# A 64 KB store of zeros ahead of the loads, in place of an early 1 MB store

## The chip, the cores and the metric

The kernel runs on one core of a Trainium2 chip. Of the core's engines it uses VectorE (DVE) for all arithmetic on the large tensors, ScalarE (ACT) for two small activations, and the queues of SyncE (SP) and ScalarE to issue DMAs; sixteen DMA engines move the data between HBM and the on-chip memory. The metric is the device time of one execution in microseconds (us), as the median over several runs. A profiled execution has besides a span, from the first to the last thing that the profiler recorded.

## The reference

```python
batch, seq, hidden, n_experts, k = 16, 1024, 512, 8, 2
...
logits_max = np.max(router_logits, axis=-1, keepdims=True)
probs = np.exp(router_logits - logits_max)
probs = probs / np.sum(probs, axis=-1, keepdims=True)
topk_indices = np.argsort(probs, axis=-1)[..., -k:]
topk_probs = np.take_along_axis(probs, topk_indices, axis=-1)
topk_probs = topk_probs / np.sum(topk_probs, axis=-1, keepdims=True)
x_expanded = x[:, :, np.newaxis, :].repeat(k, axis=2)
return (x_expanded * topk_probs[..., np.newaxis]).astype(np.float32)
```

For each of 16,384 tokens the two largest of eight router logits are turned into two weights that sum to one, and the token's 512 float32 values are written out twice, once times each weight. So 33.55 MB of x and 0.52 MB of logits are read, and 67.11 MB are written.

## The kernel before

The tokens are laid out with 128 of them on each of 128 partitions (M = 128): partition p holds tokens 128p to 128p + 127. A "row" below is one token index m on all 128 partitions. One row of x is 2 KB on each partition, and one row of the output is 4 KB on each partition.

The logits come in with one DMA (L72). `top2_weights` finds the largest and the second largest of the eight logits with a tree of maxima and minima on DVE (L26 to L36), takes their difference (L39), and two sigmoids on ACT (L41, L42) give both weights for all rows, in the tile WA.

Then two groups of 64 rows are handled one after the other (L93). For each group the SP queue issues four loads of 16 rows, 4 MB each, into the tile xs (L96), and then a plan of seven entries is walked through (L83 to L91). Each entry is one multiplication on DVE (L99), which writes n rows times both weights, and one store of those rows (L107). Where the product goes differs: rows 0 to 15 go to a second tile, osp, in two parts of e = 2 and 14 rows; rows 16 to 31 overwrite the lower half of xs, whose rows are by then used up; rows 32 to 47 go to osp again in two halves, which must first have been stored; rows 48 to 63 overwrite the upper half of xs.

Nothing is double-buffered beyond this. The loads of the second group overwrite xs, so two of them wait for the store of its lower half, and the other two for the stores of its upper half. All DMAs are issued from the SP queue, in program order, with one exception: the very first store, of rows 0 and 1 of the first group (1 MB), goes out on the ACT queue (L106). In the second group the same two rows are stored from the SP queue. A DMA's arrival is signalled by a semaphore, and the framework adds the waits on it: before an instruction that reads or overwrites a tile, before a store to output bytes that an earlier store wrote, and, since there are eight such semaphores, before the ninth DMA reuses the first one's.

Of the kernel before, what the change touches and what calls it, by code (L numbers as in the profile page):

```python
# [1 line left out]

# [4 lines left out]

F32 = mybir.dt.float32
ALU = mybir.AluOpType
ACTF = mybir.ActivationFunctionType  # L10
P = 128


def top2_weights(nc, pool, logits, M, E):

    hi, lo, n = None, None, E
    while n > 1:  # L20
        n //= 2
        if hi is None:
            a, b = logits[:, :, 0:n], logits[:, :, n : 2 * n]
            nhi = pool.tile([P, M, n], F32, tag=f"hi{n}")
            nlo = pool.tile([P, M, n], F32, tag=f"lo{n}")
            nc.vector.tensor_tensor(nhi, a, b, op=ALU.max)  # L26
            nc.vector.tensor_tensor(nlo, a, b, op=ALU.min)  # L27
        else:
            a, b = hi[:, :, 0:n], hi[:, :, n : 2 * n]
            nhi = pool.tile([P, M, n], F32, tag=f"hi{n}")  # L30
            nlo = pool.tile([P, M, n], F32, tag=f"lo{n}")
            tmp = pool.tile([P, M, n], F32, tag=f"tmp{n}")
            nc.vector.tensor_tensor(tmp, lo[:, :, 0:n], lo[:, :, n : 2 * n], op=ALU.max)  # L33
            nc.vector.tensor_tensor(nlo, a, b, op=ALU.min)  # L34
            nc.vector.tensor_tensor(nlo, nlo, tmp, op=ALU.max)  # L35
            nc.vector.tensor_tensor(nhi, a, b, op=ALU.max)  # L36
        hi, lo = nhi, nlo
    dlt = pool.tile([P, M], F32, tag="dlt")
    nc.vector.tensor_tensor(dlt, hi[:, :, 0], lo[:, :, 0], op=ALU.subtract)  # L39
    WA = pool.tile([P, M, 2], F32, tag="WA")  # L40
    nc.scalar.activation(WA[:, :, 0], dlt, ACTF.Sigmoid, scale=-1.0)  # L41
    nc.scalar.activation(WA[:, :, 1], dlt, ACTF.Sigmoid, scale=1.0)  # L42
    return WA


@with_exitstack
def kernel(
    ctx: ExitStack,
    tc: tile.TileContext,
    x: bass.AP,  # L50
    router_logits: bass.AP,
    k: bass.AP,
    out: bass.AP,
):
    nc = tc.nc
    B, S, D = x.shape
    E = router_logits.shape[-1]
    N = B * S
    assert int(k) == 2 and E == 8 and N % P == 0
    M = N // P  # L60

    GROUP = 64
    L = 16
    x_v = x.rearrange("b s d -> (b s) d").rearrange("(p m) d -> p m d", p=P)
    o_v = out.rearrange("b s k d -> (b s) k d").rearrange("(p m) k d -> p m k d", p=P)
    rl_v = router_logits.rearrange("b s e -> (b s) e").rearrange(
        "(p m) e -> p m e", p=P
    )

    wpool = ctx.enter_context(tc.tile_pool(name="wpool", bufs=1))  # L70
    logits = wpool.tile([P, M, E], F32)
    nc.sync.dma_start(logits, rl_v)  # L72
    WA = top2_weights(nc, wpool, logits, M, E)

    xs = wpool.tile([P, GROUP, D], F32)
    osp = wpool.tile([P, L, 2, D], F32)


    low = xs[:, : 2 * L, :].rearrange("p (r k) d -> p r k d", k=2)
    high = xs[:, 2 * L :, :].rearrange("p (r k) d -> p r k d", k=2)  # L80
    h = L // 2
    e = 2
    plan = [  # L83
        (0, e, osp[:, :e]),
        (e, L - e, osp[:, e:]),
        (L, L, low),
        (2 * L, h, osp[:, :h]),
        (2 * L + h, h, osp[:, h:]),
        (3 * L, h, high[:, :h]),
        (3 * L + h, h, high[:, h:]),  # L90
    ]  # L91

    for g in range(M // GROUP):  # L93
        m0 = g * GROUP
        for r in range(0, GROUP, L):
            nc.sync.dma_start(xs[:, r : r + L, :], x_v[:, m0 + r : m0 + r + L, :])  # L96
        for r, n, og in plan:
            rows = slice(m0 + r, m0 + r + n)
            nc.vector.tensor_tensor(  # L99
                og,  # L100
                xs[:, r : r + n, :].unsqueeze(2).to_broadcast([P, n, 2, D]),
                WA[:, rows, :].unsqueeze(3).to_broadcast([P, n, 2, D]),
                op=ALU.mult,
            )

            queue = nc.scalar if rows.start == 0 else nc.sync  # L106
            queue.dma_start(o_v[:, rows], og)  # L107


# [1 line left out]
_INS = ['x', 'router_logits', 'k']  # L111
_OUTS = [((16, 1024, 2, 512), 'float32')]

_NUMBERS = {'k': 2}


# [26 lines left out]
```

## Time and profile before

| | |
|---|---|
| Time, median of 6 runs | 242.74 us |
| The six runs | 241.92, 242.01, 242.70, 242.78, 242.79, 242.91 us |
| The profiled execution, time | 241.89 us |
| The profiled execution, span | 240.1 us |
| DVE busy | 142.1 us (59% of the span), 25 instructions |
| ACT busy | 1.8 us, 3 instructions |
| DMA, mean rate over the span | 421 GB/s, 101.19 MB |
| HBM read, written | 34.08 MB, 67.11 MB |

The profile names a group of instructions by its line, its engine and the tiles it writes and reads, as in "L99 DVE osp<-xs,WA". q1 is the SP queue's ring of DMA work and q10 the ACT queue's; both feed the same sixteen DMA engines. "Issue to landing" is the time from the issuing instruction to the last semaphore event of a DMA, so it includes what stands ahead of the DMA in its ring. A DMA is cut into packets; in this kernel a packet is one contiguous piece on one partition, and each of the sixteen engines handles eight partitions, so every DMA of 128 partitions is eight packets on each engine and a semaphore packet of 4 bytes. The trace keeps every packet's start, length in bytes and duration.

### The profile page before, as it was taken

To read this page: it belongs to the slowest core of one execution; us is meant where nothing else is said; L and a number is where in the kernel's file an instruction comes from. 1 tells how busy PE (TensorE), PEld (TensorE's weight loads), DVE (VectorE), ACT (ScalarE), POOL (GpSimd) and SP (SyncE) were. 2 spreads that over 40 slices of the span, in tenths; PEclk is the share of its full clock that TensorE was granted. 3 is DMA by queue.
4 is the path that set the end of the run, shared out by engine and by line. 5 is a ranking of instruction groups with operands and counts; after the bars stand their busy time and mean duration, and the time that the engine had idled before them with its cause. 6 is when DMAs were issued, how large, how long until landed. Compare 5 with 4: busy or idle time off the path is not lost.

```text
span 240.1 us, 116 instructions
## 1 busy us (share of the span) xinstructions
DVE 142.1 (59%) x25; ACT 1.8 (1%) x3; POOL 0.2 (0%) x4
## 2 busy tenths in 40 slices
DVE  2369999910499999300000999997007999990000
ACT  2000000000000000000000000000000000000000
POOL 0000000000000000000000000000000000000000
DMA  6999999989989899999999999989989898999996
GB/s 262 437 437 393 459 426 437 513 353 411 502 371 502 349 437 437 437 437 437 437 349 437 437 437 437 437 343 524 420 383 513 349 524 349 437 437 437 437 437 262
DMA packets 3312, 101.19 MB, mean 421 GB/s; under 512 B 368, under 2 KB 368, under 8 KB 496
## 3 DMA queue, kind: packets, MB, share of 16 engines
q1 hardware_dynamic: 3168, 100.14, 97.6%
q10 hardware_dynamic: 144, 1.05, 1.0%
HBM read 34.08 MB, written 67.11 MB: 421 GB/s over the span
## 4 chain that ended last, share of the span: by engine, by line
DMA 49%; DVE 32%; issue 7%; SPq 1%; DVEq 0%
DMA out_dram<-osp 26%; DMA xs<-in_x_dram 23%; DVE osp L99 18%; DVE xs L99 14%; SPq L96 0%; SPq L72 0%; SPq L107 0%; DVEq L99 0%
## 5 line engine op out<-in xcount | busy, mean ns | idle before, releaser
L99 DVE TENSOR_TENSOR osp<-xs,WA 128x8192 f32<-128x8192 f32 (+2 forms) x8 | 69.2, 8687 | 69.2 <-DMA xs<-in_x_dram 40.4
L99 DVE TENSOR_TENSOR xs<-xs,WA 128x8192 f32<-128x8192 f32 (+1 forms) x6 | 69.2, 11536 | 0.2
L26 DVE TENSOR_TENSOR nhi<-logits 128x512 f32<-128x512 f32 x1 | 0.7, 691 | 4.5 <-DMA logits<-in_router_logits_dram 4.5
L41 ACT ACT_TABLE_LOAD x1 | 1.3, 1283 | 0.7 <-PEq L124 0.7
L33 DVE TENSOR_TENSOR tmp<-nlo 128x256 f32<-128x256 f32 (+1 forms) x2 | 0.7, 352 | 0.0
L34 DVE TENSOR_TENSOR nlo<-nhi 128x256 f32<-128x256 f32 (+1 forms) x2 | 0.7, 352 | 0.0
L36 DVE TENSOR_TENSOR nhi<-nhi 128x256 f32<-128x256 f32 (+1 forms) x2 | 0.7, 352 | 0.0
L35 DVE TENSOR_TENSOR nlo<-nlo,tmp 128x256 f32<-128x256 f32 (+1 forms) x2 | 0.7, 352 | 0.0
L27 DVE TENSOR_TENSOR nlo<-logits 128x512 f32<-128x512 f32 x1 | 0.7, 684 | 0.0
L41 ACT ACTIVATE WA<-dlt 128x128 f32<-128x128 f32 x1 | 0.3, 315 | 6.2 <-DVE dlt L39 6.2
L39 DVE TENSOR_TENSOR dlt<-nhi,nlo 128x128 f32<-128x128 f32 x1 | 0.3, 292 | 0.0
L42 ACT ACTIVATE WA<-dlt 128x128 f32<-128x128 f32 x1 | 0.3, 298 | 0.0
L124 POOL MEMSET const-bfloat16-1.0<- 128x1 bf16 x1 | 0.1, 102 | 0.0
L124 POOL MEMSET const-uint8-127<- 128x1 uint8 x1 | 0.1, 102 | 0.0
L124 POOL MEMSET const-float32-1.0<- 128x1 f32 x1 | 0.1, 99 | 0.0
L124 POOL MEMSET const-float32-0.0<- 128x1 f32 x1 | 0.1, 98 | 0.2 <-issue 0.2
## 6 DMA issues: line engine op xcount, KB each, us to landing
xs<-in_x_dram SPq DMA_DIRECT2D x8, 4096.0 KB, 36.7
out_dram<-osp SPq DMA_DIRECT2D x4, 4096.0 KB, 20.7
out_dram<-xs SPq DMA_DIRECT2D x4, 4096.0 KB, 22.7
out_dram<-osp SPq DMA_DIRECT2D x2, 7168.0 KB, 31.6
out_dram<-osp ACTq DMA_DIRECT2D x1, 1024.0 KB, 16.2
out_dram<-osp SPq DMA_DIRECT2D x1, 1024.0 KB, 29.7
logits<-in_router_logits_dram SPq DMA_DIRECT2D x1, 512.0 KB, 3.7
out_dram<-xs SPq DMA_DIRECT2D x2, 33.6
```

What stands on the lines that cost most here:

```text
L26: nc.vector.tensor_tensor(nhi, a, b, op=ALU.max)
L27: nc.vector.tensor_tensor(nlo, a, b, op=ALU.min)
L33: nc.vector.tensor_tensor(tmp, lo[:, :, 0:n], lo[:, :, n : 2 * n], op=ALU.max)
L34: nc.vector.tensor_tensor(nlo, a, b, op=ALU.min)
L35: nc.vector.tensor_tensor(nlo, nlo, tmp, op=ALU.max)
L36: nc.vector.tensor_tensor(nhi, a, b, op=ALU.max)
L39: nc.vector.tensor_tensor(dlt, hi[:, :, 0], lo[:, :, 0], op=ALU.subtract)
L41: nc.scalar.activation(WA[:, :, 0], dlt, ACTF.Sigmoid, scale=-1.0)
L42: nc.scalar.activation(WA[:, :, 1], dlt, ACTF.Sigmoid, scale=1.0)
L99: nc.vector.tensor_tensor(og, xs[:, r : r + n, :].unsqueeze(2).to_broadcast([P, n, 2, D]), WA[:, rows, :].unsqueeze(3).to_broadcast([P, n, ...
L124: nc = _bacc.Bacc("TRN2", target_bir_lowering=False, num_devices=1)
```

## The change

Before the logits are loaded, a small tile `blank` of 128 floats on each partition is set to zero on DVE, and the ACT queue stores it over the first 128 values of output row 0, first copy, on every partition (128 pieces of 512 bytes, 64 KB in all). The split of rows 0 to 15 into 2 and 14 is gone from the plan, in both groups: there are six entries, and rows 0 to 15 are one multiplication and one store of 8 MB. All proper stores are issued from the SP queue. The zeros are overwritten by the first of these stores.

```diff
     wpool = ctx.enter_context(tc.tile_pool(name="wpool", bufs=1))
+
+
+    blank = wpool.tile([P, 128], F32)
+    nc.vector.memset(blank, 0.0)
+    nc.scalar.dma_start(o_v[:, 0, 0, :128], blank)
+
     logits = wpool.tile([P, M, E], F32)
     nc.sync.dma_start(logits, rl_v)
     WA = top2_weights(nc, wpool, logits, M, E)
...
     h = L // 2
-    e = 2
     plan = [
-        (0, e, osp[:, :e]),
-        (e, L - e, osp[:, e:]),
+        (0, L, osp),
         (L, L, low),
...
                 op=ALU.mult,
             )
-
-            queue = nc.scalar if rows.start == 0 else nc.sync
-            queue.dma_start(o_v[:, rows], og)
+            nc.sync.dma_start(o_v[:, rows], og)
```

## The prediction

> **What bounds the kernel now.** I read the slices of the span first, then the rings, then who waits. The DMA row of the slices and the rings:
>
> ```profile
> DVE  2369999910499999300000999997007999990000
> ...
> DMA  6999999989989899999999999989989898999996
> ...
> q1 hardware_dynamic: 3168, 100.14, 97.6%
> q10 hardware_dynamic: 144, 1.05, 1.0%
> ```
>
> DVE has holes of 10 to 34 us; the DMA engines have none. The two rings' packets fill 97.6 + 1.0 = 98.6% of 240.1 us = 236.7 us of each engine. The packet records give the rest: the first data packet starts at 2.0 us, the last ends at 239.15 us, and between them no engine is idle. So the span is 2.0 of start, 237.1 of packets on the slowest engine, and 0.95 behind the last packet. DVE and the queues only matter if they leave the rings empty. Who waited:
>
> ```profile
> DVE osp L99 <- DMA xs<-in_x_dram: 40.4, 2, 34.3
> DVE osp L99 <- DMA out_dram<-osp: 28.8, 2, 14.4
> ACT WA L41 <- DVE dlt L39: 6.2, 1, 6.2
> DVE nhi L26 <- DMA logits<-in_router_logits_dram: 4.5, 1, 4.5
> ```
>
> DVE waits for DMA, 69 us in all; these are waits behind a full ring. The chain that ended last confirms it only half (DMA 49%, DVE 32%), because it steps through DVE wherever a wait ended there; the packet records decide.
>
> **How much lead the first stores have.** The timeline and the SP queue's own lines:
>
> ```profile
> 14.26 17.29 DVE L99 TENSOR_TENSOR osp<-xs,WA 128x2048 f32<-128x2048 f32 x2 [6.03 <-DMA xs<-in_x_dram]
> 16.58 0.37 ACTq L107 DMA_DIRECT2D out_dram<-osp  x1
> 31.57 0.35 SPq L107 DMA_DIRECT2D out_dram<-osp  x1
> ...
> 132.30 17.29 DVE L99 TENSOR_TENSOR osp<-xs,WA 128x2048 f32<-128x2048 f32 x2 [34.34 <-DMA xs<-in_x_dram]
> 134.62 15.34 SPq L107 DMA_DIRECT2D out_dram<-osp  x2
> ```
>
> Four loads are queued at the start; their last semaphore packets come at 45.7 to 46.0 us, in the second group at 161.0 to 161.7 us. The early store of the second group is issued at 134.6 us but moves only from 161 us on, behind the loads: it brings nothing there. The one on ACT does overtake, and merely pushes 2.5 us of loads back.
>
> **The change, part by part.** The unit is packet time on one DMA engine, since that is what the span is made of.
>
> *Packets of the split.* In the window from 20 to 40 us the ACT ring shows
>
> ```profile
> q10 hardware_dynamic: 144, 1.05, 12.4%
> ```
>
> 12.4% of 20 us = 2.48 us for 9 packets per engine: eight of 8 KB at 0.309 us and a semaphore packet of 0.009. The 14-row store takes 8 x 2.116 us, and the 16-row store that is already there (rows 16 to 31) 8 x 2.418. Merging saves 8 x (0.309 + 2.116 - 2.418) + 0.009 = 0.065 us a group, **-0.13 us** for both.
>
> *The blank store.* Not in the trace. A 64 KB packet runs at 27.1 B/ns; at that rate 4 KB needs 0.151 us and 8 KB 0.302, and they take 0.159 and 0.309, so a packet has some 8 ns of its own. 512 bytes are then 19 + 8 = 27 ns, eight 0.22 us, with the semaphore packet **+0.22 us**. It can't be below the bytes alone, 64 KB / 434 GB/s = 0.15. Against this stands the Trainium skill, "DMA: Bandwidth & Descriptors", section Bandwidth: its measured table gives a 64 KB transfer 0.95 us, and its rules call anything under 64 KB mostly overhead, which speaks against this change. The same table gives 1 MB 6.15 us, where the row above shows 2.48 for 1 MB inside full rings. Its figures are [...]from GpSimd and in the load direction; here the engines have other packets to go on with. I take 0.22; with 0.95 the sum below would be +0.8 instead of +0.1.
>
> *Turns between loads and stores.* Load packets of 32 KB last 1.213 us, except in four places where the records show more. As excess per engine (sum over the packets / 16): 0.25 us at the start (first logits packets, up to 0.92 us instead of 0.16); 0.54 us at 18.4 to 23.5, around the ACT store's first packets; 0.02 us at 44.4, before the 14-row store; 1.28 us at 118.6 to 126, where stores give way to loads; 0.51 us at 158.0 to 160.1, before the second group's early store. The change removes the 0.54. The loads now meet their first large store near 43 us: like 158 us (loads for long, then a store: 0.51) or like 44 us (a large-packet store: 0.02). I take 0.51, since at 44 us a store had just been running. The second group's turn keeps 0.51 for the same reason, with 0.02 as its low end. Sum: -0.54 + 0.51 + 0 = **-0.03 us**, from -1.01 (both 0.02) upward. The blank is itself a store among loads: by its bytes, 1/16 of the ACT store's 0.54, **+0.03**, at most 0.54.
>
> *Off the path.* The memset on DVE costs at most what 128x128 operations there cost (0.29 us), at 0.7 us, while DVE waits for the logits until 4.46. On ACT it is queued first: wait for the memset, issue of 0.37 (the row of L107), then the table load of 1.28 and the first sigmoid, so the table is there near 2.7 us, and it is needed at 8.26. Uncovered, these would be 0.7 us. Logits and loads land 0.2 us later through the blank's packets; the weights are ready at 8.8 us with the first load needed till 14.26. The first multiplication now is one of 17.22 us instead of two in 17.29, so the 8 MB store is issued near 31.7 us, and with 1.3 us from issue to first packet (logits: 0.73 to 2.0) it stands in the ring at 33, 10 us before the loads run out. In the second group it is issued at 149.6 and loads last to 161: again 10 us. If that cover were gone, each us beyond would be a us of idle DMA. SP issues one DMA less (0.33 us). The first store now also waits for the zeros to land, since it rewrites those bytes; behind it on SP stand all later stores and loads. The blank should land by 6 us, as the logits did at 4.5, and the wait is over 25 us before it is reached. The reuse of rows 32 to 47's buffer waits for one 8 MB store instead of the 7 MB one; it ends at the same place in the ring, 63 us.
>
> *Sum:* -0.13 + 0.22 - 0.03 + 0.03 = +0.09 us. Span 240.1 -> 240.2, profiled time 241.89 -> 242.0. The six runs fall into two groups, two near 242.0 and four at 242.7 to 242.9; the profiled one belongs to the lower. Its time is 0.85 below the median, and I put the same difference on the sum: **242.8 us**.
>
> **Rivals.**
> 1. *The small packets made the turns.* Both 0.5 us stalls stand ahead of 8 KB packets, the 56 KB packets at 44 us had 0.02. If size is the cause, both turns shrink to 0.02: 242.74 - 1.01 - 0.13 + 0.25 = 241.85. For it: exactly this coincidence. Against it: the stalls fall on load packets up to 3 us before the first 8 KB packet, and the worst turn, 1.28 us, has none.
> 2. *Slower: a turn straight into a full store is the dear kind.* If the two turns near 43 and 160 us cost what the turn at 118 us does, 1.28 each, the sum is +0.09 + 2 x 0.77 = 1.6, so 244.4 us. It decides (over 0.3%, 0.73 us) from 0.83 us a turn. For it: such a turn exists, in large packets. Against it: its direction is the other one, and 44 us shows a large store with none.
> 3. *The blank is dear at the start,* by the page's 0.95 us or because it holds up every engine's first reads once more (0.75 us, as four of them showed): +0.8 to +0.9, 243.6 us.
> 4. *The zeros don't come first, or do nothing:* the ACT queue issues them near 1 us, beside the logits rather than ahead of them. Same time as the forecast.
>
> **How the numbers follow.** Within 0.3% of 242.74, about what a measurement of this kernel can tell from no change, is 242.0 to 243.5. Forecast with rival 4: 0.60, nearly all inside. Rival 1: 0.17, mostly beyond 242.0, and a median out of the lower group of runs adds a little. Rivals 2 and 3: 0.11 and 0.12, nearly all slower. So faster 0.18, same 0.60, slower 0.22. The range runs from rival 1 (241.8) to rival 3 (243.7); outside are most of rival 2 and some below.
>
> **What would show it.** The rings' shares should again fill 98 to 99%; q10 with 144 packets and 0.07 MB; the first 8 MB store landing near 63 us; DVE's waits on loads and on osp the same to 0.5 us. In the packet records: 512-byte packets of 27 ns; no long load packets at 18 to 24 us; 0.5 us of them near 43 and 160. Wrong it would be by empty rings near 43 or 161 us, by 512-byte packets of 0.1 us or more, by turns over 0.8 us, or by a first store that waits for the zeros.

## The result

The changed kernel takes 242.58 us (median of 31 runs) against 242.05 for the kernel before (68 runs). The ratio is 1.0021, 95% interval 1.0016 to 1.0027: 0.5 us slower, inside the 0.3% that was called no change. The profiled execution took 242.17 us with a span of 240.4, which no other of the 31 was below; its trace shows 0.3 us of the 0.5.

The page after: the DVE and DMA rows of the slices, and the rings.

```profile
DVE  2359999920499999300000999998008999990000
...
DMA  7999999898989899999999999999999898999996
...
q1 hardware_dynamic: 3024, 101.19, 98.5%
q10 hardware_dynamic: 144, 0.07, 0.1%
```

The rings are again full, 98.6% of the span, and q10 holds the zeros alone. Who waited, after:

```profile
DVE osp L103 <- DMA xs<-in_x_dram: 40.7, 2, 34.3
DVE osp L103 <- DMA out_dram<-osp: 28.7, 2, 14.4
ACT WA L41 <- DVE dlt L39: 5.6, 1, 5.6
DVE nhi L26 <- DMA logits<-in_router_logits_dram: 3.6, 1, 3.6
```

DVE's two large waits have kept their size to 0.3 us. The timeline of the start and of the first store:

```profile
0.73 0.37 SPq L78 DMA_DIRECT2D logits<-in_router_logits_dram  x1
0.82 0.17 DVE L74 MEMSET blank<- 128x128 f32 x1 [0.82 <-PEq L126]
1.02 0.41 ACTq L75 DMA_DIRECT2D out_dram<-blank  x1
1.15 2.12 SPq L100 DMA_DIRECT2D xs<-in_x_dram  x4
1.46 1.28 ACT L41 ACT_TABLE_LOAD   x1 [1.46 <-DVE blank L74]
...
14.80 17.23 DVE L103 TENSOR_TENSOR osp<-xs,WA 128x16384 f32<-128x16384 f32 x1 [6.46 <-DMA xs<-in_x_dram]
32.05 0.35 SPq L109 DMA_DIRECT2D out_dram<-osp  x1
```

The zeros go out at 1.02 us, beside the logits. The table load ends at 2.74 us and is needed at 8.37. The SP queue's own waits before its stores are:

```profile
SPq L109 <- DVE osp L103: 115.4, 6, 27.2
SPq L109 <- DMA out_dram<-blank: 1.5, 1, 1.5
```

With its loads issued, SP stands 1.5 us until the zeros have landed, near 4.8 us, and then 27.2 us more for the multiplication. So the wait for the zeros costs nothing, and the first proper store follows the multiplication at 32.05 us. The loads' last semaphore packets come at 43.3 to 43.9 us, so the store stands ready behind them for some ten microseconds.

What differs is in the durations of the DMA packets. Each packet size has a duration that most of its packets keep; what single packets take beyond it, summed and divided by 16 engines, is called the stall of that stretch. In this table "first turn" is where the first group's loads give way to its stores (40 to 53 us, without the early store itself), "back" is where loads resume (118 to 127 us), and "second turn" is the second group's (157 to 161 us). Times are us per engine, each from one trace.

```
kernel             at the early store  first turn  back  second turn  ratio to before
before             0.54                0.02        1.28  0.51         1
after              -                   0.51        1.32  0.26         1.0021
no_early           -                   1.21        0.91  0.53         1.0020
late_blank         -                   0.88        0.77  0.62         1.0028
late_blank2        -                   0.98        1.28  0.36         1.0022
early_on_sp        -                   1.07        1.36  0.32         1.0015
both               0.63                0.00        1.13  0.63         1.0003
split_first        0.69                0.00        0.95  0.77         0.9997
early_both_groups  0.63                0.00        1.47  0.21 *       0.9987
early_1_row_both   0.13                0.63        0.88  0.53         0.9994
early_8_rows       1.05                1.13        0.91  0.44         1.0064
dve_half_more      -                   0.00        1.26  0.62         0.9996
* at 137 to 141 us, at its early store; none near 160
```

### The profile page after: what moved, and what is told of

It reads as the page before. It is cut to its first block, busy times and chain, and to the rows that moved or that the text cites. A ratio compares the mean times of both kernels' runs of the same rounds, so it can differ in the third digit from the quotient of the medians.

```text
span 240.4 us, 115 instructions
## 1 busy us (share of the span) xinstructions
DVE 142.1 (59%) x24; ACT 1.8 (1%) x3; POOL 0.2 (0%) x4
## 4 chain that ended last, share of the span: by engine, by line
DMA 46%; DVE 36%; issue 7%; SPq 0%; DVEq 0%
DMA out_dram<-osp 26%; DVE osp L103 22%; DMA xs<-in_x_dram 20%; DVE xs L103 14%; SPq L78 0%; SPq L109 0%; DVEq L103 0%
## 5 line engine op out<-in xcount | busy, mean ns | idle before, releaser
L103 DVE TENSOR_TENSOR osp<-xs,WA 128x8192 f32<-128x8192 f32 (+1 forms) x6 | 69.0, 11534 | 69.4 <-DMA xs<-in_x_dram 40.7
```

The lines of the kernel that those rows point to most:

```text
L103: nc.vector.tensor_tensor(og, xs[:, r : r + n, :].unsqueeze(2).to_broadcast([P, n, 2, D]), WA[:, rows, :].unsqueeze(3).to_broadcast([P, n, ...
```

## The experiments

All are timed against the kernel before, in the same session.

**The zeros, and the early store, one at a time.** In `no_early` the zeros are taken out of the changed kernel; in `both` they are put into the kernel before.

```diff
# no_early, from the changed kernel
-    blank = wpool.tile([P, 128], F32)
-    nc.vector.memset(blank, 0.0)
-    nc.scalar.dma_start(o_v[:, 0, 0, :128], blank)
# both, from the kernel before
+    blank = wpool.tile([P, 128], F32)
+    nc.vector.memset(blank, 0.0)
+    nc.scalar.dma_start(o_v[:, 0, 0, :128], blank)
```

> The changed kernel without the store of zeros: six entries in the plan, nothing early. Theory B (the blank costs the time, by 0.22 us of packets and the 0.40 us more stall on load packets at the start that the trace after shows): the time falls to 242.05 - 0.13 = 241.9 us, 0.2 to 0.3% below the changed kernel, and the stall at the start is back near 0.26 us per engine. Theory E (the early 1 MB store was worth something by itself, and the zeros change little): about 242.4 us, and the stall at the start stays where the run happens to put it. Turn near 42 us: 0.5 us per engine by both.

> The kernel before with the store of zeros added and nothing removed. Theory B: 242.05 + 0.22 + 0.40 = 242.7 us, ratio about 1.0026. Theory E: 242.05 + 0.1 to 0.2 = 242.2 us at most, ratio below 1.001. The turns at 18 to 24, 44, 118 and 158 us as in the kernel before.

`no_early`: 242.39 us against 241.85, ratio 1.0020 (1.0011 to 1.0029). `both`: 242.13 us, ratio 1.0003 (0.9993 to 1.0014). The two answer alike: with or without the zeros the kernel that has no early 1 MB store is 0.2% slower, and the zeros alone add 0.07 us (-0.17 to 0.34) to the kernel before. Theory B, which I had formed on the 0.40 us more stall at the start of the trace after, falls as the account of the time. The stall at the start differs from trace to trace: 0.11 to 0.81 us (mean 0.47) in the eight traces of this study that have loads in the same order and no zeros at the start, 0.60 to 1.16 (mean 0.87) in the five that have them. So the traces lean towards a dearer start with zeros; the times of `both` leave room for 0.34 us at most.

**One group only.** `split_first` leaves the split and the early store to the first group.

```diff
-        for r, n, og in plan:
+        parts = plan if g == 0 else [(0, L, osp)] + plan[2:]
+        for r, n, og in parts:
```

> The kernel before with the second group's rows 0 to 15 whole; the first group keeps its split and the early store on the ACT queue. By the packet sum -0.07 us, and the turn near 160 us between 0.26 (as in the trace after) and 0.51 (as in the trace before): 241.7 to 242.0 us. If small packets make the stalls ahead of them (rival 1), the turn near 160 us falls to 0.02 us and the time to 241.5.

Measured 241.85 us, ratio 0.9997 (0.9987 to 1.0007). The second group's split was worth nothing. Its turn, now straight into a store of 64 KB packets, took 0.77 us per engine, not 0.02: the stall doesn't need small packets.

**The zeros at another time.** `late_blank` moves the line that stores them behind the weights:

```diff
-    nc.scalar.dma_start(o_v[:, 0, 0, :128], blank)
...
     WA = top2_weights(nc, wpool, logits, M, E)
+    nc.scalar.dma_start(o_v[:, 0, 0, :128], blank)
```

> The changed kernel with its store of zeros issued behind the two sigmoids on the ACT queue (near 9 us), in the middle of the loads, and not at the start. If the dear part is that the zeros meet the first reads at the start, the start's stall is back at 0.26 us per engine and the time is 242.0 + 0.22 = 242.2 us or less. If any small store among loads is dear, the stall moves to 9 to 14 us, 0.3 to 0.5 us per engine, and the time stays at 242.5.

242.57 us against 241.85, ratio 1.0028 (1.0018 to 1.0039). This run does not test what it was meant to: the framework orders by what an instruction needs, and issued the zeros at 1.02 us on ACT all the same. It is the changed kernel a second time, with a first turn of 0.88 us. `late_blank2`, from the kernel without zeros, makes them depend on the weights:

```diff
+    blank = wpool.tile([P, 64, 2], F32)
+    nc.vector.tensor_tensor(blank, WA[:, :64, :], WA[:, :64, :], op=ALU.subtract)
+    nc.scalar.dma_start(o_v[:, 0, 0, :128], blank.rearrange("p a b -> p (a b)"))
```

> The changed kernel with its zeros computed from the weights (weights minus themselves, one more VectorE operation of about 0.2 us), so that the 64 KB store goes out on the ACT queue near 9 us, in the middle of the loads. If a small early store among loads is enough to soften the later turn (theory C or M at any size): 242.05 + 0.1, ratio below 1.001, and less than 0.3 us per engine near 42 us. If the softening needs the 1 MB or its lateness: ratio 1.002 to 1.003, as with the zeros at the start, and 0.5 to 1.2 us near 42.

They now go out at 9.21 us, and the time is 242.66 us against 241.99, ratio 1.0022 (1.0014 to 1.0031). 64 KB among the loads does not do what 1 MB did; the first turn is 0.98 us.

**Split without overtaking.** `early_on_sp`:

```diff
-            queue = nc.scalar if rows.start == 0 else nc.sync
-            queue.dma_start(o_v[:, rows], og)
+            nc.sync.dma_start(o_v[:, rows], og)
```

> The kernel before, with its first 1 MB store on the SP queue like all others: the split of rows 0 to 15 stays, but the store stands behind the loads and overtakes none. Theory M (what the change gave up is that the early store's packets run among the loads, which makes the later change from loads to stores cheap): ratio near 1.002, as with no early store, and a stall of 0.5 to 1.2 us per engine near 42 us. Theory S (the split itself, small first packets, is what helped): ratio 1.000.

242.48 us against 241.99, ratio 1.0015 (1.0008 to 1.0022), first turn 1.07 us. The kernel issues the same DMAs at the same sizes as the kernel before, and only the ring of one differs. The split itself is worth nothing; letting the 1 MB run among the loads is worth about 0.15%.

**The same in both groups.** `early_both_groups`:

```diff
-            queue = nc.scalar if rows.start == 0 else nc.sync
+            queue = nc.scalar if r == 0 else nc.sync
```

> The kernel before, with the 1 MB store of the second group's first two rows on the ACT queue too, so that it runs among the loads from 136 us. Theory M: the turn near 160 us (0.26 to 0.77 us per engine in six traces) goes and a smaller stall comes near 137 us, as in the first group; the time falls by 0.2 to 0.5 us, ratio 0.998 to 0.999. Theory C (only the first store of all matters, something paid once): ratio 1.000.

241.78 us against 241.99, ratio 0.9987 (0.9978 to 0.9997): ahead of both kernels, by the least effect that these runs can tell. Its timeline in the second group, and the rings from 130 to 152 us:

```profile
132.63 17.29 DVE L99 TENSOR_TENSOR osp<-xs,WA 128x2048 f32<-128x2048 f32 x2 [34.72 <-DMA xs<-in_x_dram]
134.95 0.34 ACTq L107 DMA_DIRECT2D out_dram<-osp  x1
149.95 0.34 SPq L107 DMA_DIRECT2D out_dram<-osp  x1
```

```profile
q1 hardware_dynamic: 288, 8.39, 89.2%
q10 hardware_dynamic: 144, 1.05, 11.3%
```

The 1 MB now moves before the loads are over (all 144 of its packets lie in this stretch). A stall of 0.21 us comes with it, and the one at 160 us is gone.

**How much is to run among the loads.** `early_1_row_both` stores one row early (512 KB) in both groups; `early_8_rows` stores eight (4 MB) in the first.

```diff
# early_1_row_both
-    e = 2
+    e = 1
-            queue = nc.scalar if rows.start == 0 else nc.sync
+            queue = nc.scalar if r == 0 else nc.sync
# early_8_rows
-    e = 2
+    e = 8
```

> The kernel before with an early store of one row instead of two (512 KB, packets of 4 KB), on the ACT queue in both groups. Theory X: half the bytes among the loads, about half the stall at 18 to 24 us (0.3 us per engine), with the turn near 44 us still small: ratio 0.997 to 0.999. If the softening of the turn scales with the bytes: a turn of 0.3 us or more near 44 us, and ratio 1.000.

> The kernel before with rows 0 to 15 split into 8 and 8 in place of 2 and 14: the store on the ACT queue is 4 MB in packets of 32 KB, issued near 23 us, and runs among the loads for most of the rest of them. Rival 1 of the prediction (8 KB packets make the stalls ahead of them): the stall at the early store and the one at 160 us go to 0.02 us per engine each, ratio 0.996 to 0.998. Theory X (what stalls load packets is stores running among them, and it grows with how much runs so): 0.54 us grows to 1 to 2 us per engine, ratio 1.002 to 1.006.

One row: 241.84 us against 241.82, ratio 0.9994 (0.9983 to 1.0006). Its early stalls are small (0.13 and 0.01 us), but the turns behind them are there again, 0.63 and 0.52. Its time is as good as that of the kernel before all the same, so the stall of the first turn does not set the time by itself. Eight rows: 243.43 us, ratio 1.0064 (1.0045 to 1.0083), with 1.05 us at the early store and 1.13 at later places, and not an 8 KB packet in the kernel. Its ACT ring from 20 to 40 us:

```profile
q10 hardware_dynamic: 91, 2.98, 34.5%
```

A third of the stretch is stores among loads, and the stall grew with it, as theory X had it. All stalls of this trace come to 4.25 us, 1.6 more than before, and the time is 1.6 us longer.

**All loads on the other ring.** `loads_on_act` takes the changed kernel without zeros and issues the loads of x from ACT:

```diff
-            nc.sync.dma_start(xs[:, r : r + L, :], x_v[:, m0 + r : m0 + r + L, :])
+            nc.scalar.dma_start(xs[:, r : r + L, :], x_v[:, m0 + r : m0 + r + L, :])
```

> The changed kernel without the zeros, with all eight loads of x on the ACT queue and all stores on SP, so that loads and stores overtake each other in both groups, the second group's loads among the first group's stores too. Theory M: all turns soften, the one near 118 us (0.8 to 1.3 us per engine) as well: ratio 0.995 to 0.998. If mixing costs as much as it saves: 1.000 to 1.003, with stalled load packets spread over the whole of the mixed stretches.

255.00 us against 241.99, ratio 1.0524 (1.0500 to 1.0548): a miss for both theories. The DMA row, the waits, and four windows (length, busy time of DVE, ACT and POOL, clock, DMA share, GB/s), and behind them the third window in the kernel before:

```profile
DMA  7929999899999999999999999999999999999993
```

```profile
ACT WA L41 <- DVE dlt L39: 14.4, 1, 14.4
DVE nhi L26 <- DMA logits<-in_router_logits_dram: 13.0, 1, 13.0
```

```profile
5.00:11.00 6.00, 0.00 (x0) 0.00 (x0) 0.00 (x0) 1.00 1.01 433
11.00:20.00 9.00, 6.41 (x12) 0.51 (x2) 0.00 (x0) 1.00 0.52 203
35.00:70.00 35.00, 16.81 (x1) 0.00 (x0) 0.00 (x0) 1.00 1.02 381
70.00:97.00 27.00, 22.06 (x3) 0.00 (x0) 0.00 (x0) 1.00 0.98 422
```

```profile
35.00:70.00 35.00, 20.59 (x2) 0.00 (x0) 0.00 (x0) 1.00 1.04 449
```

The span of this trace is 12.8 us longer than before, in three parts. Where loads and stores ran interleaved, from 35 to 70 us, packets stalled by 4.8 us per engine and the rate was 381 GB/s, against 449 before; all stalls together were 9.1 us, 6.5 more than before. Then the logits came at 13 us instead of 4.5, the first sigmoid waited for them, and three loads were queued behind it on ACT: the rings were empty from 13.3 to 13.8 us until 17.8 to 18.6, 4.6 us on the mean of the engines. The rest, 1.8 us, is that the last engine ended 2.2 us behind the mean of the sixteen, against 0.4 before.

**The cover.** `dve_half_more` does half of the changed kernel's first multiplication twice, `dve_twice` all of it.

```diff
# dve_half_more (the first group's first entry)
+            if rows.start == 0:
+                nc.vector.tensor_tensor(og[:, :h], ..., op=ALU.mult)
# dve_twice
+            for _ in range(2 if rows.start == 0 else 1):
                 nc.vector.tensor_tensor(og, ..., op=ALU.mult)
```

> The changed kernel with 8.7 us of VectorE work more (half of the first multiplication done twice), so that the first 8 MB store is issued near 40.5 us. By the prediction's cover (10 us between the store's packets being ready and the loads' end) nothing is lost: the changed kernel's 242.5 us, ratio to before 1.002 to 1.003. If the cover is less than 8.7 us: the difference is added as idle DMA near 43 us.

> The changed kernel with its first multiplication done twice (17.2 us more on VectorE): the first store is issued near 49 us, its packets start near 50 us, and the loads end near 43. By the prediction's cover of 10 us, 7 us of DMA are idle and the time is 242.5 + 7 = 249.5 us, ratio about 1.03; later stores must not fall behind any further. If the first multiplication's time mattered in itself, it would be 17 us more.

`dve_twice` took 249.47 us, ratio 1.0317 (1.0296 to 1.0338), as worked out from the cover. Its window from 43 to 51 us, in the same columns:

```profile
43.00:51.00 8.00, 7.96 (x2) 0.00 (x0) 0.00 (x0) 1.00 0.31 131
```

The share counts a packet whole in the window in which it starts, so sixteen store packets of 2.4 us that start at 50.8 to 50.9 us are in the 31%. By the packet records the rings are empty from the loads' last semaphore packets (42.9 to 44.0 us) until then, 7.6 us on the mean of the engines, in a run that was the slowest of the five (250.45 us). `dve_half_more` surprised me. It does more work than the changed kernel and took 241.69 us against 241.82, ratio 0.9996 (0.9982 to 1.0010), where the changed kernel has 1.0021 (1.0016 to 1.0027). Its store of 8 MB is issued late:

```profile
23.93 17.23 DVE L110 TENSOR_TENSOR osp<-xs,WA 128x16384 f32<-128x16384 f32 x1
41.18 0.35 SPq L116 DMA_DIRECT2D out_dram<-osp  x1
```

In `dve_twice`, with nothing ahead in the ring, the first packet came 0.84 us after the issue (49.95 to 50.79). So this store is ready near 42.0 us, when the loads' last semaphore packets are only 1.0 us off (43.0 to 43.8), and its trace has no stall at the first turn. That fits where the stall lies in the other traces: almost wholly on the last two load packets of each engine (1.21 of `no_early`'s 1.21 us). Of these two, one had started on every engine (40.6 to 41.4 us) before this store was ready. Whether that is the reason is not shown. The trace of `dve_half_more` is of the slowest of its 14 runs (242.84 us, with 1.16 us of stall at the start), so only its times say that it is fast.

## Why the prediction was right, and where it was off

It forecast no change and 242.8 us; the median is 242.58 and the ratio 1.0021, a small loss that is clear of noise. Its sum gave +0.1 us where +0.5 was measured. By its steps:

- **What bounds.** Right: rings full at 98.6% before and after, and 17.2 us more on DVE (`dve_twice`) cost about 7 us, because 10 us of them were covered. Its packet times are 0.24 us late against the profile's clock: the first data packet of the kernel before starts at 1.76 us and the last ends at 238.91, and its 1.3 us from issue to first packet are 1.0. The cover stays, since both of its ends move alike. The shortest of DVE's waits for x or osp is 6 us (6.03, the row at 14.26), not 10.
- **Packets of the split, -0.13 us.** The 64 KB packets took 2.418 us, as assumed. Too small to be seen in a time: `split_first`, which has half of it, is at 0.9997 with 0.1% to either side.
- **The zeros, +0.22 + 0.03 us.** The 512-byte packets took 27 ns each, as worked out. In time they cost 0.07 us in `both` (-0.17 to 0.34), and nothing between `no_early` and the changed kernel (1.0020 and 1.0021). The 0.95 us for 64 KB in the Trainium skill, "DMA: Bandwidth & Descriptors", section Bandwidth, is outside the interval of `both`: it is not what this store cost.
- **Turns, -0.03 us.** This is the term that was mis-sized, and by the prediction's own sign of being wrong (turns over 0.8 us) it failed in four of five traces. The trace after did show 0.51 us at the first turn, but that was the lowest of five: without a 1 MB store among the loads it came to 0.51, 0.88, 0.98, 1.07 and 1.21, mean 0.93; with one, the early store's stall and the turn together came to 0.56, 0.63, 0.63 and 0.69, mean 0.63. So the term is +0.30 at this turn. By the times it is larger: `no_early` is 0.48 us slower (0.27 to 0.70) though its packets are 0.13 less, which leaves 0.4 to 0.8. What the rest is, the traces tell only in part. In the same nine traces all stalls behind the start come to 2.49 us on the mean without the early store and 2.37 with it, so the other turns make up for some of the 0.30. The semaphore packets of the last store end 0.21 us later on the mean of the engines (238.75 against 238.54), and the last engine is 0.21 us further behind that mean (0.64 against 0.43); two of the five traces, `late_blank` and `late_blank2`, make that second difference. So it is shown that the early store among the loads is worth about 0.2%; that the stall of the first turn is the way in which it acts is argued.
- **Off the path.** Memset 0.17 us (at most 0.29 was allowed), table ready at 2.74 (2.7), weights at 8.9 (8.8), first store at 32.05 (31.7), its landing at 63.56 (63). Only the SP queue waited for the zeros, 1.5 us that ended 27 us before the first store.
- **The base.** The six runs shown put the median at 242.74, and I read two groups into them. 68 runs have it at 242.05, with most between 241.8 and 242.2: no two groups, and my 0.85 us for the difference was wrong. From 242.05 the same sum gives 242.1, 0.4 below the measured time. That the base made up for the turn is luck.
- **Rivals.** 1 (small packets make the turns) is refuted by `split_first` and `early_8_rows`. Of 2 the size comes true at the first turn, 0.93 on the mean against the 0.83 from which it was to decide, but the second turn stayed at 0.26 to 0.77. 3 (dear zeros) is refuted by `both`. 4 holds in its first half: the zeros are issued beside the logits.

Open is why a store that stands ready behind loads for ten microseconds makes their last packets slow, when one that comes at the loads' end, or follows 1 MB that ran among them, doesn't; and why one row early leaves the turn at 0.63 us and two rows don't. One row was through the ring at 30.7 us and two at 32.5; the next store was issued at 31.8 and 31.6 and so ready some 0.8 us later. No run varied that alone.

## What to carry to other kernels

When the DMA engines are full from end to end, work moved on other engines is free up to its cover, and here that cover could be worked out from the trace to a microsecond. What is left is how loads and stores meet: here 1 MB of stores among 16 MB of loads gained 0.2% against none, and 4 MB lost 0.6% against 1 MB. An effect of this size needs each part undone by itself and many runs, since one trace's stall of a turn varied between 0.5 and 1.2 us.

## What the runs showed of the hardware that I had not expected

- In these traces two rings take turns packet by packet, though the packets' lengths differ. In `loads_on_act` the logits' eight 4 KB packets on each engine lay 1.365 us apart (the median), one load packet (1.213) plus one of their own (0.159) to within 0.01, so 0.5 MB took 12 us. The early store's 8 KB packets in the kernel before lay 1.52 us apart likewise (1.213 + 0.309).
- Stores running among loads slow the packets: 0.13 us for 0.5 MB, 0.54 to 0.69 for 1 MB, 1.05 for 4 MB, 4.8 us in 35 us of full mixing.
- More work ahead of a store made a kernel faster than its parent, 0.9996 (0.9982 to 1.0010) against 1.0021 (1.0016 to 1.0027). The store then came when the loads were all but done; that this is what helped is argued from a single trace without a stall there.
